# Thirty-four seven-product couples a layer in a two-layer encoder trunk, with block sums made by adding transfers

## The chip, the cores and the metric

One core of one Trainium2 chip runs the whole trunk in one launch. The metric is the time of an execution on the device in microseconds; the median of the runs counts, lower is better. Five engines work side by side: PE (matrix products), DVE (vector), ACT (scalar), POOL (GpSimd) and SP, which here only issues transfers. Each executes its own instructions in order and waits at semaphores for the others.

## The reference

The input is 256 tokens of width 2048, in float32. There are two layers. Layer 0 mixes tokens with a bidirectional mLSTM of 8 heads, layer 1 with a bidirectional gated linear recurrence (HGRN2) of 16 heads. After each mixer stands a ConvGLU of inner width 5504.

```python
def conv_glu(hn, w_up, conv_w, conv_b, w_down):
    u = hn @ w_up
    a, v = jnp.split(u, 2, axis=-1)
    ...
    return (jax.nn.gelu(c, approximate=False) * v) @ w_down

for layer in range(DEPTH):
    hn = rmsnorm(h, norm_mix_g[layer])
    ...
    h = h + mix
    h = h + conv_glu(rmsnorm(h, norm_ffn_g[layer]), ...)
return rmsnorm(h, final_g)
```

In `conv_glu`, `c` is `a` convolved over three neighbouring tokens, plus a bias. The change concerns the last product of `conv_glu`, 256 x 5504 by 5504 x 2048.

## The kernel before, in words

**Products.** Every float32 operand is split into a high and a low part (`wh`, `wl` for weights, two halves of a tile for activations), and a product is three matmuls: high by high, high by low, low by high. Weights come from DRAM in `raw` tiles of 2048 columns (1 MB, three buffers); `parts` makes pieces of 1024 columns from them, the high part by a copy on ACT, the low part by a subtraction on DVE. `stream` takes pieces three ahead of PE's use (LOOK).

**Chunks.** The work is a list of chunks. "fm" is 256 output features for all tokens, "tm" is 512 output features with the tokens as rows, "st" is a pair of such 512s.

**Pairs.** In a pair (`pair`, `squares_by_seven`), two 128-row slices of the contraction and two 512-column blocks form, with the two token halves, a product of 2 x 2 by 2 x 2 blocks. Such a couple takes eight products, or seven by a Strassen-like scheme (Winograd's form). The seven need sums of token blocks, which `token_sums` makes when the activation is produced, and sums T1 to T4 of weight blocks B11, B22, B21, B12. A pair holds all eight banks of PSUM: four for P1, P6, P7, P5 (`psm`), which `mid` adds to the residual after the last couple of seven, and four for C11, C12, C21, C22 (`psa`), which `done` adds at the end. `SEVEN` lists the couples of seven of the feed-forward stage, `SEVEN_MIX` those of the mixers' out projections, whose weight sums are made on the fly by DVE (`combine`).

**The feed-forward stage** (`ffn`) goes through its 43 tiles of inner width in two halves, of 22 (FA) and 21 (FB). Each half has one fm chunk per tile (`w_up`), whose `done_up` makes the activation tile. The first half then has two pairs, for output columns 0 to 1023 and 1024 to 2047, with 8 couples of seven each. The second half has one pair for columns 0 to 1023, with 6 couples of seven, and then two single tm chunks, for columns 1024 to 1535 and 1536 to 2047 (chunks 2 and 3, `w_d2`). That makes 22 couples of seven a layer. Their weight sums are made in the up chunks before them by `prepare`: it loads the four blocks into `pwh` and `pwl`, DVE does four operations of 512 columns, and the result goes to DRAM (`tscr`). `split_squares` later loads 768 KB of weights, 768 KB of sums into `T`, and 256 KB of sums into the free quarter of `raw`.

**Order.** Program order is written by generators. `Side` holds jobs, each with a due time on a clock that `tick` moves by 0.65 for each pair of matmuls in an fm chunk (10.4 a chunk of 16 slices) and by 1.3 for each slice of a tm chunk (20.8 a chunk of 16). A job's `yield 9.0` puts its next instructions 9 later on this clock. `until` and `drain` step the jobs at once, whatever their due time. A scheduler may still move instructions, except those that are pinned (`pin`, `late`), which keep their order. After out projection chunk 0 of a mixer, `mixed` calls `drain`.

**The norms.** `Norm.add(c)` squares the 512 columns of chunk c on ACT and pushes `turn(c)`, which transposes them on PE and makes four activation tiles `xt` for the next stage, one ACT and one DVE instruction each. `turn` waits while a pair holds the banks (`held`). The next stage's products start with tile 0 and take the tiles in order. The last norm (`FinalNorm`) scales and stores; `half` is its end, run for each token half inside the last chunk.

Of the kernel before, what the change touches and what calls it, by code (L numbers as in the profile page):

```python
# [46 lines left out]
LEAD = 48  # L47
TEMP = 3
GATES = 4 * AH
SEVEN = (1, 2, 3, 4, 6, 7, 8, 9), (1, 2, 4, 5, 7, 8)  # L50
# [6 lines left out]
C_ID, C_MF, C_MB, C_SUM, C_LV = 0, 128, 384, 640, 768  # L57
NCST = C_LV + FINE * QUAD


def trunk_kernel(ctx, tc, xT, x_d, fg_d, pp_d, cst_d, w_gate, w_first, w_aq, w_ak, w_av, w_ao, w_aout, w_ao2,
                 w_bq, w_bv, w_bg, w_bout, w_bo2, w_up, w_d0, w_d1, w_d2, out, mscr, tscr):
# [10 lines left out]
    cst = keep.tile([P, NCST], F32, name="cst")  # L73
# [45 lines left out]
    class Chunk:  # L119
        def __init__(self, kind, src, nk, x, done, before=None, last=False, swap=(), first=False, paced=False):  # L120
            self.last, self.swap, self.first, self.paced = last, swap, first, paced
            self.kind, self.src, self.nk, self.x, self.done, self.before = kind, src, nk, x, done, before
            self.width = {"fm": 256, "tm": 512, "st": 512}[kind]
# [57 lines left out]
    def split_squares(ch, parts):  # L181

        units, raws, kept = (ch.nk + 1) // 2, {}, {}
        side.until(lambda: ch.waits is None or ch.waits)
# [11 lines left out]
        def combine(u):  # L196
            r, T = raw(u), temporary(ch.pool, "T")
            B11, B22, B21, B12 = (r[:, j * 512:(j + 1) * 512] for j in range(4))
            T2, T3, T4 = (T[:, j * 512:(j + 1) * 512] for j in range(3))
            for x, y, out in ((B12, B22, T3), (B12, B11, B12), (B22, B12, T2), (B21, T2, T4)):  # L200
                dve.tensor_tensor(out, x, y, ALU.subtract)
            kept[u] = T
# [16 lines left out]
    def squares_by_seven(ch, fetch, ready):  # L219
# [18 lines left out]
        units, last = (ch.nk + 1) // 2, max(ch.seven)  # L238
        for u in range(units):
            fetch()  # L240
# [43 lines left out]
    def stream(chunks):  # L284
# [10 lines left out]
        for ch in chunks:  # L295
# [7 lines left out]
            while k < ch.nk:  # L303
                fetch()
                wh, wl, n = ready.pop(0)
                if ch.last and k + sum(p[2] for p in ready) + n == ch.nk:
                    pieces_, k0 = [(wh, wl, n)] + ready, k
                    for t in range(2):
                        k = k0
                        for wh, wl, n in pieces_:  # L310
                            for kk in range(n):
                                x, c = ch.x(k), slice(kk * 512, (kk + 1) * 512)
                                xh, xl = x[:, t * P:(t + 1) * P], x[:, T + t * P:T + (t + 1) * P]
                                pe.matmul(ps[t], xh, wh[:, c], start=False, stop=False)
                                pe.matmul(ps[t], xh, wl[:, c], start=False, stop=False)
                                pe.matmul(ps[t], xl, wh[:, c], start=False, stop=k == ch.nk - 1)
                                k += 1
                        ch.half(ps[t], t)
                    return
# [129 lines left out]
    class FinalNorm:  # L449
# [17 lines left out]
        def scale(self, c):  # L467
# [5 lines left out]
            if c == 2:  # L473
                ss = self.ss
                dve.tensor_tensor(ss[:, :, 0:1], ss[:, :, 0:1], ss[:, :, 1:2], ALU.add)
                dve.tensor_tensor(ss[:, :, 0:1], ss[:, :, 0:1], ss[:, :, 2:3], ALU.add)
                dve.tensor_scalar(self.rc, ss[:, :, 0], 1.0 / D, EPS, ALU.mult, ALU.add)

        def half(self, ps, t):
            side.drain()  # L480
            cs = slice(D - 512, D)
            h = hm[:, t, cs]
            dve.tensor_tensor(h, h, ps, ALU.add)
            last = keep.tile([P, 512], F32, tag=f"xt{4 + t}", name="fl")
            dve.scalar_tensor_tensor(last, h, 1.0, h, ALU.mult, ALU.mult, accum_out=self.ss[:, t, 3:4])
            rc = self.rc[:, t:t + 1]
            dve.tensor_scalar(rc, self.ss[:, t, 3:4], 1.0 / D, rc, ALU.mult, ALU.add)
            pool.tensor_tensor(rc, rc, hmx[:, 0:1], ALU.pow)
            for c in range(4):
                v = hm[:, t, 512 * c:512 * c + 512]  # L490
                if c in (1, 2):
                    act.activation(v, v, AF.Copy, scale=rc)
                elif c == 3:
                    dve.scalar_tensor_tensor(v, v, rc, self.g[3], ALU.mult, ALU.mult)
                else:
                    dve.tensor_scalar(v, v, rc, None, ALU.mult)
                (nc.scalar if c == 2 else nc.sync).dma_start(out[t, :, 512 * c:512 * c + 512], v)
# [11 lines left out]
    def project(wsrc, nk, x, norm):  # L509

        def done(c):
            def f_(ps):
# [3 lines left out]
                if norm is not None:  # L516
                    norm.add(c)
            return f_
        chunks = [Chunk("tm", wsrc(c), nk, x, done(c)) for c in range(4)]
        if isinstance(norm, FinalNorm):  # L520
            chunks[3].last, chunks[3].half = True, norm.half
        return chunks
# [6 lines left out]
    def token_sums(mp, i, a, b, S, last=None):  # L529
# [3 lines left out]
        for i, (x, y, op) in enumerate(((a[:, P:T], b[:, P:T], ALU.add), (a[:, P:T], a[:, 0:P], ALU.subtract),  # L533
                                        (S[:, 0:P], a[:, 0:P], ALU.subtract), (b[:, 0:P], S[:, 2 * P:3 * P], ALU.subtract))):
# [8 lines left out]
    def pair(src, nk, c0, x, sums, norm, seven):  # L543
# [5 lines left out]
        def mid(ps):  # L549
# [6 lines left out]
            dve.tensor_tensor(part(0, 1), part(0, 1), u, ALU.add)  # L556
            dve.tensor_tensor(part(1, 1), part(1, 1), P5, ALU.add)
            dve.tensor_tensor(u, u, P7, ALU.add)  # L558
            pool.tensor_tensor(part(1, 0), part(1, 0), u, ALU.add)  # L559
            pool.tensor_tensor(part(1, 1), part(1, 1), u, ALU.add)  # L560

        def done(ps):
            for i in range(4):
# [12 lines left out]
        ch.stored, ch.waits, ch.pool = {}, None, None  # L576
        return ch

    def prepare(mp, todo, period, finished):
# [13 lines left out]
        for i, (_, dst) in enumerate(todo):  # L593
# [3 lines left out]
            for x, y, out in ((B12, B22, B22), (B12, B11, B12), (B11, B22, B11), (B21, B11, B21)):  # L597
                dve.tensor_tensor(out, x, y, ALU.subtract)  # L598
# [3 lines left out]
        finished.append(True)  # L602
# [33 lines left out]
    def mlstm(norm, nxt):  # L636
# [10 lines left out]
        def load(loaded, follower):  # L647
# [26 lines left out]
            late(cst[:, 0:C_LV], cst_d[:, 0:C_LV])  # L674
# [8 lines left out]
        def begin():  # L683
            c = stack.enter_context(tc.tile_pool(name="cols", bufs=1))
            box["cc"] = c.tile([P, 2, H], F32, name="cc")
            box["emn"] = c.tile([P, 2, H], F32, name="emn")
            mp = box["mp"] = stack.enter_context(tc.tile_pool(name="ml", bufs=1))
# [5 lines left out]
        def gates(gs):  # L693
            with tc.tile_pool(name="gt", bufs=1) as gp:
# [3 lines left out]
                pe.matmul(pg[:, 0:T], cst[:, C_SUM:C_SUM + P], gs, start=True, stop=True)  # L698
# [45 lines left out]
        segs = [  # L744
            (0, 256, 0, 0, 0, cst[:, C_MF:C_MF + 256]),
            (256, 384, 1, 0, 128, cst[:, C_MF:C_MF + 128]),
            (384, 512, 0, 1, 0, cst[:, C_MB + 128:C_MB + 256]),
            (512, 768, 1, 1, 0, cst[:, C_MB:C_MB + 256]),
        ]

# [8 lines left out]
        def weights(hd):  # L759
# [6 lines left out]
            for lo, hi, s, dr, t0, mk in segs:  # L766
# [5 lines left out]
        def head(st, j):  # L772
# [7 lines left out]
            for lo, hi, s, dr, t0, mk in segs:  # L780
# [132 lines left out]
    def hgrn(norm, nxt):  # L913
# [4 lines left out]
        def begin():  # L918
            mp = box["mp"] = stack.enter_context(tc.tile_pool(name="hg", bufs=1))
            late(cst[:, C_LV:], cst_d[:, C_LV:])  # L920
# [193 lines left out]
    def ffn(layer, norm, nxt):  # L1114
        stack = ExitStack()
        box = dict(n=(2 * len(SEVEN[0]) + len(SEVEN[1])) * layer)
        chunks, pairs = [], []
# [9 lines left out]
        def done_up(f, i, GT, SX, seven):  # L1127
            def go(ps):
# [18 lines left out]
                if i % 2 and i // 2 in seven:  # L1147
                    n = seven.index(i // 2)
                    if seven is SEVEN[0]:
                        z = GT[i - 1][:, P:T], GT[i - 1][:, T + P:2 * T]  # L1150
                    else:
                        if n % 3 == 0:
                            box["s4"] = mp.tile([P, 768], F32R, tag=f"sx{len(seven) + n // 3}", name="s4")
                        z = tuple(box["s4"][:, (n % 3 * 2 + j) * P:(n % 3 * 2 + j + 1) * P] for j in range(2))
# [4 lines left out]
        for part, (f0, nf) in enumerate(((0, FA), (FA, FB))):  # L1159
            GT, SX, todo, finished = [], {}, [], []  # L1160

            def prep(todo=todo, finished=finished, nf=nf):
                if not pairs[0].pool:
                    begin()
                side.push(prepare(box["mp"], todo, (nf * 10.4 - 26.0) / len(todo), finished))

            for i in range(nf):
                chunks.append(Chunk("fm", w_up[layer, f0 + i], KT, norm.x, done_up(f0 + i, i, GT, SX, SEVEN[part]),
# [146 lines left out]
```

## Time and profile before

| | |
|---|---|
| median of 3 runs | 2397.41 us |
| the runs | 2397.41, 2397.83, 2393.29 us |
| span of the profiled execution, first to last instruction | 2388.1 us |
| what lies around the span, against the median | 9.3 us |
| PE busy | 2371.3 us, 99% |
| DVE busy | 1939.6 us, 81% |
| ACT busy | 1352.4 us, 57% |
| POOL busy | 189.7 us, 8% |
| moved by DMA | 578.15 MB, mean 242 GB/s |

The profile is of one execution; the times of its parts are read against its own span. A row of a group gives the count, the busy time and the mean duration of one, then the idle time of the engine before them and what ended it. A row of waits gives the total, how often and the longest. A row of the chain or of the timeline gives its start, its length and how many instructions it merges. PE's granted clock is full in nearly all of the span, 0.999 in the mean.

### The profile page before, as it was taken

To read this page: it belongs to the slowest core of one execution; us is meant where nothing else is said; L and a number is where in the kernel's file an instruction comes from. 1 tells how busy PE (TensorE), PEld (TensorE's weight loads), DVE (VectorE), ACT (ScalarE), POOL (GpSimd) and SP (SyncE) were. 2 spreads that over 40 slices of the span, in tenths; PEclk is the share of its full clock that TensorE was granted. 3 is DMA by queue.
4 is the path that set the end of the run, shared out by engine and by line. 5 is a ranking of instruction groups with operands and counts; after the bars stand their busy time and mean duration, and the time that the engine had idled before them with its cause. 6 is when DMAs were issued, how large, how long until landed. Compare 5 with 4: busy or idle time off the path is not lost.

```text
span 2388.1 us, 38126 instructions
## 1 busy us (share of the span) xinstructions
PE 2371.3 (99%) x14596; PEld 2027.1 (85%) x14596; DVE 1939.6 (81%) x3167; ACT 1352.4 (57%) x2141; POOL 189.7 (8%) x240
## 2 busy tenths in 40 slices
PE   9999999999999999999999999999999999999998
PEld 7888888888788888888888888888888878888887
DVE  7766687888888888767888989889788888888874
ACT  7655455555565555655555555556555566455563
POOL 0100000000000000001222222220000000000000
PEclk9999999999999999999999999999999999999999
DMA  8654546998987777755544554545798998777774
GB/s 301 201 183 163 185 184 226 324 322 323 330 340 277 271 247 242 277 190 182 177 162 175 177 175 164 175 173 190 277 324 326 333 359 310 265 244 249 246 273 143
DMA packets 105703, 578.15 MB, mean 242 GB/s; under 512 B 11936, under 2 KB 12448, under 8 KB 58672
## 3 DMA queue, kind: packets, MB, share of 16 engines
q1 hardware_dynamic: 103824, 571.71, 67.5%
q0 software_dynamic: 1120, 3.21, 0.7%
q8 instruction: 114, 1.87, 0.3%
q10 hardware_dynamic: 576, 0.79, 0.1%
q14 instruction: 69, 0.57, 0.1%
HBM read 527.37 MB, written 48.30 MB: 241 GB/s over the span
## 4 chain that ended last, share of the span: by engine, by line
PE 90%; DMA 6%; DVE 3%; issue 1%; ACT 0%; SPq 0%; POOLq 0%; POOL 0%; DVEq 0%; ACTq 0%
PE mm L330 32%; PE mm L346 23%; PE mm L334 16%; PE pc L229 10%; PE mm L229 5%; DMA pwl<-in_w_d 2%; DVE wl L143 1%; DMA T<-tscr 1%; DMA pwh<-in_w_d 1%; PE pn L793 1%; PE py L1051 1%; DMA tscr<-pwl 1%; PE pd L1001 0%; PE pz L407 0%; PE pa L1001 0%
## 5 line engine op out<-in xcount | busy, mean ns | idle before, releaser
L330 PE MATMUL mm<-xt,wh 128*128 128x512 f32 x3776 | 1314.0, 394 | 0.0
L143 DVE TENSOR_TENSOR wl<-raw,wh 128x1024 fp32r<-128x1024 f32 (+1 forms) x846 | 1033.4, 1227 | 268.7 <-ACT wh L142 265.3
L142 ACT CAST wh<-raw 128x1024 fp32r<-128x1024 f32 (+1 forms) x846 | 874.4, 1040 | 567.1 <-PE mm L330 265.6
L334 PE MATMUL mm<-xt,wl 128*128 128x256 f32 x3776 | 1046.6, 278 | 1.1 <-DVE wl L143 1.1
L330 PEld LDWEIGHTS mm<-xt,wh 128*128 128x128 f32 x3776 | 706.2, 188 | 159.3
L334 PEld LDWEIGHTS mm<-xt,wl 128*128 128x128 f32 x3776 | 709.5, 188 | 6.5 <-DVE wl L143 2.0
L346 PE MATMUL mm<-wh,xt 128*128 128x512 f32 x1024 | 320.6, 391 | 1.8 <-ACT xt L352 1.3
L346 PEld LDWEIGHTS mm<-wh,xt 128*128 128x128 f32 x1024 | 191.5, 188 | 42.0 <-ACT xt L352 1.7
L346 PE MATMUL mm<-wl,xt 128*128 128x512 f32 x512 | 198.2, 391 | 0.0
L229 PE MATMUL pc<-wh,g 128*128 128x512 f32 x576 | 195.1, 390 | 0.3 <-ACT wh L142 0.2
L229 PEld LDWEIGHTS pc<-wh,g 128*128 128x128 f32 x576 | 108.0, 188 | 24.8 <-ACT wh L142 2.0
L229 PE MATMUL pc<-wl,g 128*128 128x512 f32 x288 | 112.3, 390 | 0.9 <-DVE wl L143 0.9
L346 PEld LDWEIGHTS mm<-wl,xt 128*128 128x128 f32 x512 | 96.2, 188 | 18.9
L143 DVE TENSOR_TENSOR wl<-T,wh 128x1024 fp32r<-128x1024 f32 (+1 forms) x100 | 93.8, 951 | 21.7 <-ACT wh L142 21.3
L229 PE MATMUL mm<-wh,sx 128*128 128x512 f32 x300 | 107.1, 391 | 2.8 <-ACT wh L142 2.8
L142 ACT CAST wh<-T 128x1024 fp32r<-128x1024 f32 (+1 forms) x100 | 82.3, 835 | 45.7 <-PE pc L229 23.3
L559 POOL TENSOR_TENSOR hm<-hm,u 128x512 f32<-128x512 f32 x8 | 11.2, 1399 | 1151.6 <-DVE u L558 1151.6
L1138 ACT ACTIVATE avc<-avc,pp 128x256 f32<-128x256 f32 x86 | 51.6, 600 | 87.7 <-DVE avc L1136 87.7
L346 PE MATMUL mm<-wh,g 128*128 128x512 f32 x308 | 96.5, 392 | 0.0
L1133 ACT COPY avc<-mm 128x256 f32<-128x256 f32 x172 | 63.7, 371 | 51.4 <-PE mm L334 50.9
L598 DVE TENSOR_TENSOR pwl<-pwl 128x512 f32<-128x512 f32 x88 | 60.2, 684 | 27.9 <-DMA pwl<-in_w_d 27.9
L598 DVE TENSOR_TENSOR pwh<-pwh 128x512 f32<-128x512 f32 x88 | 60.2, 684 | 27.8 <-DMA pwh<-in_w_d 21.6
(256 smaller groups left out, 2504.3 us busy)
## 6 DMA issues: line engine op xcount, KB each, us to landing
raw<-in_w_up SPq DMA_DIRECT2D x172, 1024.0 KB, 6.1
raw<-in_w_bq SPq DMA_DIRECT2D x48, 1024.0 KB, 4.9
raw<-in_w_d SPq DMA_DIRECT2D x40, 1024.0 KB, 5.2
raw<-in_w_d SPq DMA_DIRECT2D x44, 768.0 KB, 6.7
T<-tscr SPq DMA_DIRECT2D x44, 768.0 KB, 8.0
raw<-in_w_ao SPq DMA_DIRECT2D x24, 1024.0 KB, 4.6
pwh<-in_w_d SPq DMA_DIRECT2D x44, 512.0 KB, 8.1
pwl<-in_w_d SPq DMA_DIRECT2D x44, 512.0 KB, 7.7
```

The costliest lines, as they stand in the source:

```text
L142: pin(act.copy(wh[:, :m], r))
L143: pin(dve.tensor_tensor(wl[:, :m], r, wh[:, :m].bitcast(F32), ALU.subtract))
L229: pe.matmul(ps, a, b, start=id(ps) not in begun, stop=stop and i == 2)
L330: pe.matmul(ps[f], wh[:, c:c + P], x, start=k + kk == 0, stop=False)
L334: pe.matmul(ps[f][:, 0:T], wl[:, c:c + P], x[:, 0:T], start=False, stop=k + kk == ch.nk - 1)
L346: pe.matmul(ps[t], x[:, a + t * P:a + (t + 1) * P], w[:, c], start=st and i == 0, stop=sp and i == 2)
L559: pool.tensor_tensor(part(1, 0), part(1, 0), u, ALU.add)
L598: dve.tensor_tensor(out, x, y, ALU.subtract)
L793: pe.matmul(pn[:, 0:258], w, v, start=(i == 0), stop=(i == len(parts) - 1))
L1051: pe.matmul(py[:, c], AT[:, s if s == t else 2 + s], V[:, s, j * P:(j + 1) * P], start=(s == 0), stop=(s == 1))
L1133: act.copy(z, p[:, T:2 * T])
L1138: act.activation(c, a, AF.Identity, bias=col("conv_b", layer * FT + f), scale=cw[1])
```

## The change

The first half's two pairs have 9 couples of seven instead of 8 each. The second half's chunks 2 and 3 become a pair as well, and both its pairs have 8 couples of seven, the first one instead of 6. That makes 34 a layer. The last couple of the last pair of all, and the single slice after it, are taken bank by bank (`tail`), and `FinalNorm.bank` replaces `half`.

Of the 34 couples, four (couple 5 of each pair, `FLY`) are summed on the fly. The sums of the other 30 are stored in DRAM. The first 14 of them are made during the mixer before (`prepare_by_transfers`): a copy of the four blocks in DRAM on SP's queue, then four transfers from POOL's queue that add in DRAM, where T2 reads T3's result and T4 reads T2's. These are pinned. 9 are made by DVE in the first half's up chunks, 7 in the second half's. Signs change so that every sum is an addition. Each pair waits only for its own sums. `done` adds C11, C21, C12, C22 in this order. The mLSTM's masks leave the kept constants and are loaded when the mLSTM begins, into memory that the start-up held.

```diff
-SEVEN = (1, 2, 3, 4, 6, 7, 8, 9), (1, 2, 4, 5, 7, 8)
+SEVEN = (1, 2, 3, 4, 5, 6, 7, 8, 9), (1, 2, 3, 4, 5, 6, 7, 8)
+FLY = 5
+STORED = 2 * (len(SEVEN[0]) + len(SEVEN[1]) - 2)
+BY_TRANSFERS = 14
+FIRST = 9
+PERIOD = 28.0
...
-        side.until(lambda: ch.waits is None or ch.waits)
+        side.until(lambda: not ch.waits)
...
+        def tail(u):
+            fetch()
+            p, q, r = (ready.pop(0)[:2] for _ in range(3))
+            x0, x1, x2 = (ch.x(2 * u + i) for i in range(3))
+            ws = ((block(p, 0), block(q, 0), block(r, 0)), (block(q, 1), block(p, 1), block(r, 1)))
+            for i, ps in enumerate(psa_):
+                for x, w in zip((x0, x1, x2), ws[i % 2]):
+                    product(ps, half(x, i // 2), w, x is x2)
+                ch.bank(ps, i)
...
-            for i in range(4):
+            for i in (0, 2, 1, 3):
                 h = part(i // 2, i % 2)
                 dve.tensor_tensor(h, h, ps[i], ALU.add)
...
+    def prepare_by_transfers(todo):
+        def unit(src, dst, left):
+            late(dst, src)
+            T2, T3, T4, T1 = (dst[:, j * 512:(j + 1) * 512] for j in range(4))
+            B11, B12 = src[:, 0:512], src[:, 1536:2048]
+            yield 12.0
+            for out, in_ in ((T3, B12), (T1, B11), (T2, T3), (T4, T2)):
+                tc.keep_in_program_order(pool.dma_start(out, in_, accum_op=ALU.add))
+                if out is not T3:
+                    yield 9.0
+            left.pop()
+        for job in todo:
+            while held:
+                yield 1.0
+            side.push(unit(*job))
+            yield PERIOD
...
+            masks = box["masks"] = c.tile([P, NCST - NKEPT], F32, name="masks")
+            late(masks, cst_d[:, NKEPT:])
...
+                jobs = todo[BY_TRANSFERS:][0:FIRST] if part == 0 else todo[BY_TRANSFERS + FIRST:]
+                side.push(prepare(box["mp"], jobs, (nf * 10.4 - 26.0) / len(jobs)))
...
+            for c0, src in ((0, w_d0[layer][:, f0 * 1024:(f0 + nf) * 1024]), (2, w_d1[layer][:, f0 * 1024:(f0 + nf) * 1024])):
+                ch = pair(src, nf, c0, lambda k, GT=GT: GT[k], lambda u, SX=SX: SX[u], nxt if part else None, seven)
+                ch.waits = []
                 for u in seven:
+                    if u != FLY:
+                        ch.stored[u] = tscr[box["n"]]
+                        ch.waits.append(True)
+                        todo.append((src[:, 2048 * u:2048 * (u + 1)], tscr[box["n"]], ch.waits))
...
-                chunks += project(lambda c: w_d2[layer, c % 2], nf, lambda k, GT=GT: GT[k], nxt)[2:]
...
-    c, close0 = ffn(0, n1, n2)
+    c, close0, chunks[2].before = ffn(0, n1, n2)
...
-    c, close1 = ffn(1, n3, nf)
+    d, close1, c[1].before = ffn(1, n3, nf)
```

165 lines of the change are left out of this document (68 added, 97 removed).

## The prediction

> **What bounds the kernel now.** I read the page's head first, then the waits of PE, the chain, the windows by stage, and last the places that the change touches.
>
> ```profile
> span 2388.1 us, 38126 instructions
> PE 2371.3 (99%) x14596; PEld 2027.1 (85%) x14596; DVE 1939.6 (81%) x3167; ACT 1352.4 (57%) x2141; POOL 189.7 (8%) x240
> PE 90%; DMA 6%; DVE 3%; issue 1%; ACT 0%; SPq 0%; POOLq 0%; POOL 0%; DVEq 0%; ACTq 0%
> PE mm L229 <- ACT wh L142: 2.8, 2, 1.5
> PE mm L346 <- ACT xt L352: 1.3, 1, 1.3
> 743.92 5.89 PE pc L229 x26
> 1073.07 22.69 PE mm L346 x100
> ```
>
> PE is busy for 2371.3 of 2388.1 us; only 16.8 us are not matmul, and the largest wait of PE in total is 2.8 us. So work taken from PE pays in full, if nothing else comes late. What one matmul costs is read from the chain and not from its mean duration (390 ns, which overlaps the next): 100 in 22.69 us and 26 in 5.89 us, 0.227 us each.
>
> The stages, by window (us, then busy time and count of PE, PEld, DVE, ACT, POOL, then granted clock, DMA share, GB/s):
>
> ```profile
> 0.00:300.00 300.00, 297.43 (x1715) 252.51 (x1716) 208.50 (x387) 179.71 (x303) 15.93 (x37) 1.00 0.60 207
> 323.00:370.00 47.00, 47.00 (x209) 38.94 (x208) 45.18 (x63) 26.75 (x33) 3.54 (x2) 1.00 0.54 195
> 394.00:636.00 242.00, 240.91 (x1388) 209.96 (x1387) 207.26 (x343) 131.52 (x209) 0.00 (x0) 1.00 0.90 319
> 636.00:691.00 55.00, 52.72 (x231) 42.62 (x231) 47.55 (x57) 38.94 (x49) 0.00 (x0) 1.00 0.97 367
> 691.00:746.00 55.00, 54.91 (x242) 45.16 (x241) 47.04 (x49) 34.30 (x39) 4.35 (x2) 1.00 0.84 303
> 978.00:1033.00 55.00, 55.00 (x251) 45.79 (x250) 42.83 (x50) 34.12 (x43) 0.00 (x0) 1.00 0.76 273
> 1033.00:1061.00 28.00, 28.00 (x133) 23.19 (x132) 18.07 (x23) 15.27 (x26) 3.55 (x2) 1.00 0.50 173
> 1090.00:1588.00 498.00, 497.70 (x4472) 429.23 (x4471) 434.21 (x889) 273.72 (x520) 138.11 (x175) 1.00 0.50 174
> 1611.00:1657.00 46.00, 46.00 (x205) 38.09 (x204) 45.27 (x66) 25.54 (x32) 2.52 (x2) 1.00 0.54 197
> 1920.00:1980.00 60.00, 58.10 (x255) 45.96 (x254) 51.66 (x64) 41.44 (x52) 0.00 (x0) 1.00 0.96 367
> ```
>
> In order: the mLSTM heads, its paired out projection, the first half's up chunks of layer 0, its two pairs, the second half's pair and then one single chunk, the HGRN heads, its paired out projection, and the first pair of layer 1. PE is full everywhere but in the first pair of each layer: 2.3 us missing at 636 and 1.9 at 1920, where the DMA engines are at 0.97 and 0.96. The mixers have DMA to spare (0.60 and 0.50).
>
> **1. Products removed.** A couple in seven products instead of eight saves one, which is three matmuls. First half: 9 instead of 8 couples in each of two pairs, 2 saved. Second half: the pair goes from 6 to 8, 2 saved; chunks 2 and 3 now take 21 x 6 x 2 = 252 matmuls, as a pair 8 x 7 + 2 x 8 + 4 = 76 products or 228, which is 8 products less. 12 a layer, 24 in all: 72 x 0.227 = **-16.3 us**. This is PE time with nothing behind it.
>
> **2. The boundary between layer 0 and the HGRN.** Today the norm's transposes and tiles of columns 0 to 1023 run under single chunk 2, those of chunk 2 under chunk 3, and only chunk 3's are late. After, the second pair holds all of them until it ends, because a turn waits while a pair has the four banks. So 16 tiles are made at the moment when the next chunk wants them.
>
> ```profile
> 1072.25 0.82 PE L407 MATMUL pz<-cst,hm 128*128 128x128 f32 x6
> 1095.38 0.39 PE L346 MATMUL mm<-wh,g 128*128 128x512 f32 x1
> 1095.60 0.39 PE L330 MATMUL mm<-xt,wh 128*128 128x512 f32 x1
> 1101.51 0.84 ACT L352 ACTIVATE xt<-pz,pp 128x256 fp32r<-128x256 f32 x2 [0.42 <-PE pz L407]
> L353 DVE SCALAR_TENSOR_TENSOR xt<-pz,pp,xt 128x256 fp32r<-128x256 f32 x48 | 21.4, 478 | 3.1 <-ACT xt L352 3.1
> L501 ACT ACTIVATE jk<-hm 128x512 f32<-128x512 f32 x38 | 23.9, 630 | 3.1 <-POOL hm L560 1.6 <-DVE hm L565 0.3 <-DVE hm L515 0.3
> ```
>
> Now there is no gap: the last matmul of chunk 3 starts at 1095.38, the next chunk's first at 1095.60. After, the first tile takes transposes (0.82 for six), ACT 0.42 and DVE 0.48, with two hand-overs, about 2.5 us of idle PE. Then the tiles must keep up: the chunk lasts 242 / 22 = 11.0 us, and ACT owes 16 x 0.42 = 6.7, four squares of 0.63, 2.5, and four weight casts of about 1.04 (page: 874.4 us for 846), 4.2: 13.4 us, 2.4 over. Between 2 us (squares put off) and 9 (DVE's four additions and splits before the first tile as well); I take **+4**, near the sum of 2.5 and half of 2.4.
>
> **3. Pair after pair.** A pair's first product needs the bank of the previous pair's C11. That hand-over exists at 695 us:
>
> ```profile
> 695.80 0.19 PEld L229 LDWEIGHTS pc<-wh,g 128*128 128x128 f32 x1 [0.52 <-DVE hm L565]
> 656.67 2.35 DVE L143 TENSOR_TENSOR wl<-raw,wh 128x1024 fp32r<-128x1024 f32 x2
> 658.94 0.68 DVE L143 TENSOR_TENSOR wl<-T,wh 128x512 fp32r<-128x512 f32 x1
> 659.54 1.22 DVE L143 TENSOR_TENSOR wl<-raw,wh 128x1024 fp32r<-128x1024 f32 x1
> L598 DVE TENSOR_TENSOR pwl<-pwl 128x512 f32<-128x512 f32 x88 | 60.2, 684 | 27.9 <-DMA pwl<-in_w_d 27.9
> ```
>
> It costs 0.52 us; two new ones, and C12 now evicted third: **+1** (0 to 3).
>
> **4. DVE inside the pairs.** Back to back, DVE needs 1.135 us for a split of 1024 columns (2.27 from 656.67 to 658.94) and 0.60 for 512. A couple of seven asks three and one, 4.0 us, against 21 x 0.227 = 4.76 of PE. In the pair at 691, DVE goes from 47.04 by one couple's extra split (1.135 + 0.60) and by the couple that is now summed on the fly (four additions of 0.60) to 51.2, with PE at 54.3: 94%. The two out projections run at 45.18 of 47 and 45.27 of 46 with PE full, so 94% can be borne. But a couple on the fly wants 6.4 us of DVE in 4.76 of PE, once in each of eight pairs. **+2** (0 to 8, the last if each waits its 1 us).
>
> **5. Sums prepared by DVE.** Down from 22 to 16 a layer, 9 of them in the first half's up chunks, where there were 16: 7 x 4 x 0.60 = 17 us less DVE and 7 x 2 MB less traffic in a window at 0.90. The first pair then finds its sums stored long ago, and the 2.3 and 1.9 us missing there can shrink: **-2.5** (-4 to 0). The traffic of the new second pair, 7 x 1.79 + 3.5 MB in about 52 us, is some 315 GB/s where the single chunks drew 173; the 367 at 636 shows room, at nothing, with up to 3 us in the bound of step 4.
>
> **6. Sums made by transfers.** For each of 14 couples a layer: one 1 MB copy in DRAM on SP's queue, then four accumulating transfers of 256 KB from POOL's queue, each chained one waiting for the one before (T2 for T3, T4 for T2). 14 x 2 MB over some 280 us (from 43, the gate products and one chunk later, to 323) adds about 105 GB/s to the 207 of the mLSTM, and 59 to the HGRN's 174. No row shows an accumulating transfer; the nearest:
>
> ```profile
> fg<-in_fg POOLq DMA_DIRECT2D x4, 256.0 KB, 8.0
> Mb<-mscr POOLq DMA_DIRECT2D x16, 128.0 KB, 6.0
> raw<-tscr SPq DMA_DIRECT2D x44, 256.0 KB, 7.3
> 63.50 2.18 POOL L764 DMA_DIRECT2D Mb<-mscr  x4 [1.68 <-DMA mscr<-M]
> 366.28 1.29 POOL L559 TENSOR_TENSOR hm<-hm,u 128x512 f32<-128x512 f32 x1 [61.20 <-DVE u L558]
> ```
>
> The fourth row shows POOL itself standing until an earlier transfer has landed, before it issues; behind it stand, in order, the powers of the head norms, in the HGRN the gate products, and DVE waits for those. The program puts 9 us between chained transfers. At 8.0 us, the row of the same size and queue, POOL need not stand. The Trainium skill, "DMA: Bandwidth & Descriptors", section "Anatomy of one DMA — SWDGE (gpsimd) path", fits a GpSimd-issued transfer as 2.0 us plus bytes over 436 GB/s; an estimate by it is 2.6 us for 256 KB, the sum would be the same and the margin wide, and these rows, at 6 to 8 us, do not agree.
>
> One place has no 9 us. In side time the mLSTM offers 10.4 + 20.8 + 3 x 62.4 + 20.8 = 239 from where the transfers begin to the end of out chunk 0, and 14 x 28 = 392 are wanted; the drain at the end of that chunk sends the last five copies at once and the rest of the accumulations in a row. Five copies at 367 GB/s are 14 us in front of the paired projection's weights, of which two loads, about 11 us of PE, are already ahead: 3 us. The row of eight chained steps at 6 to 8 us is 48 to 64 us of POOL from about 312, and POOL's addition at 366.28 must follow. The HGRN offers 426 and is not drained. For all of it **+3** (0 to 25).
>
> **7. Start and end.** The masks go into memory that the start-up holds until the gate products have run.
>
> ```profile
> 29.54 1.93 PE L870 MATMUL pq<-gx,wg 128*32 128x256 f32 x32
> 41.09 0.60 PE L698 MATMUL pg<-gs,cst 128*128 128x256 f32 x2
> cst<-in_cst SPq DMA_DIRECT2D x1, 384.0 KB, 9.8
> 2379.83 0.68 DVE L483 TENSOR_TENSOR hm<-hm,mm 128x512 f32<-128x512 f32 x1
> ```
>
> Issued at 31.5, landed after 9.8 us, at 41.3, wanted at 41.09: **+0.3** (0 to 2). The end keeps its chain of addition, square, power, scaling and store, from 2379.83 to 2388.1; banks finish one by one, and one scaling moves from a plain multiply to one with a second operand: 0, within 1 either way. The new signs move no time.
>
> **Sum.** -16.3 + 4 + 1 + 2 - 2.5 + 3 + 0.3 = -8.5 us. The span would be 2379.6; the median of the three runs, 2397.41, lies 9.3 us over the span and keeps that, so 2388.9.
>
> **Rivals.** *All of it covered*: the tiles of step 2 come in time but for 2 us, the burst of step 6 is swallowed, 5 holds: about -15, 2382. For it: PE's waits are nearly nothing today though DVE is at 90% in places. Against: step 2 has no cover left.
> *The gain is turned into waits* in the mLSTM's drain and in the pairs: the second ends of steps 4 and 6 in part, 8 us more, 2397, no change. For it: eight steps of 8 us reach past 366, and an addition of DVE waits for POOL there.
> *POOL stands in the HGRN*, the slower side. If a chained accumulation takes L over 9 us, POOL stands 28 x (L - 9) us over 14 couples; DVE, which waits for POOL's products, has 498 - 434 = 64 us to spare. From L = 9 + (64 + 8.5) / 28 = 11.6 us the gain is gone; at 12 it is 84 - 64 = 20 us against 8.5, 2409. For it: an accumulation reads two operands and writes, in DRAM, beside loaded queues. Against: 8.0 us for 256 KB. The same page's section "Two DMAs through the same engine are not ordered" says that the issuing engine has to wait for the earlier transfer's semaphore; the row at 63.50 agrees.
> *The sums are not there in time*: then the pairs' loads wait behind accumulations; the drains exclude it in the program's order, so it is priced with the last.
>
> **Chances.** Forecast 0.45 (2384 to 2393), all covered 0.15, turned into waits 0.20, POOL standing 0.20. What this measurement tells from no change is about 0.2%, 4.8 us. Faster (under 2392.6) 0.60, within 0.20, slower 0.20. The range reaches from 2379, all covered and step 5 in full, to 2406, and leaves out most of the last case.
>
> **What would show it.** PE instructions down by 72; the two pairs of a second half together 2 x 52 us; after the second pair a gap of 3 to 5 us ahead of the first HGRN chunk, ended by ACT or DVE on xt; the first pairs without their 2 us; the accumulations landing in 6 to 8 us, POOL busy but not standing, PE full in the HGRN. Wrong would be: accumulations over 11 us, POOL's rows in the HGRN ended by a DMA, DVE idle for POOL, or PE idle in the paired out projection of the mLSTM.

## The result, and the profile after

The change made the kernel slower. Its median is 2432.74 us against 2395.35 for the kernel before on the same chip, a ratio of 1.0152 with a 95% interval of 1.0128 to 1.0175. The profiled execution took 2423.3 us with a span of 2421.5, 33.4 longer than the span before. The forecast was 2388.9 us, with a range of 2379 to 2406.

About 2 us lie around the span in every execution on record. Most of the 9.3 us that the table of the time before puts there are something else: the execution that was profiled took some 2390 us and was shorter than the median. The trace after is of the shortest of its four executions as well. So the parts below sum to +33.4, while the medians differ by 37.4.

The head of the page after:

```profile
span 2421.5 us, 38387 instructions
PE 2372.3 (98%) x14524; PEld 2022.9 (84%) x14524; DVE 2002.2 (83%) x3244; ACT 1392.3 (57%) x2201; POOL 291.8 (12%) x356
PE 84%; DMA 6%; DVE 5%; issue 2%; POOL 1%; ACT 1%; SPq 0%; POOLq 0%; DVEq 0%; ACTq 0%
```

The 72 matmuls are gone (14596 to 14524), and yet PE is as busy as before: matmuls after a stall run longer (up to 775 ns instead of 481 in the rows below). PE's part of the chain falls from 90% to 84%.

The two out projections are found by the tiles that only they read, `ya` (mLSTM) and `yb` (HGRN). The rows give the count, the shortest, median and longest duration in ns, then the first and last start in us. Before:

```profile
L346 PE MATMUL mm<-wh,ya x128: 387/389/481, 300.7 to 389.2; 128*128 128x512 f32 x128
...
L346 PE MATMUL mm<-wh,yb x128: 387/389/481, 1584.9 to 1677.7; 128*128 128x512 f32 x128
```

After:

```profile
L353 PE MATMUL mm<-wh,ya x128: 387/389/775, 302.7 to 423.5; 128*128 128x512 f32 x128
...
L353 PE MATMUL mm<-wh,yb x128: 387/389/498, 1622.3 to 1715.2; 128*128 128x512 f32 x128
```

The mLSTM's out projection took 88.5 us and takes 120.8. That alone is +32.3 of the 33.4. The HGRN's is unchanged (92.8 and 92.9).

The windows after, with the columns of the prediction: the mLSTM's out projection, the first pair of layer 0, the HGRN heads, the first pair of layer 1.

```profile
302.70:423.50 120.80, 96.72 (x408) 76.68 (x407) 72.81 (x105) 51.44 (x76) 27.07 (x32) 0.89 0.91 244
668.00:771.50 103.50, 103.50 (x460) 85.75 (x459) 94.70 (x106) 73.09 (x85) 3.54 (x2) 1.00 0.88 320
1121.00:1622.00 501.00, 494.59 (x4439) 424.25 (x4440) 432.40 (x879) 271.61 (x521) 186.23 (x230) 1.00 0.75 222
1960.00:2020.00 60.00, 60.00 (x268) 49.71 (x267) 55.13 (x63) 40.44 (x49) 3.55 (x2) 1.00 0.90 340
```

In the first row PE is missing 24 us, the DMA engines are at 0.91 and the granted clock at 0.89. The first pairs, rows two and four, are full now. The HGRN misses 6.4 us of PE, where it missed 0.3.

The boundary, from the timeline of PE after (start, length, and what ended the idle time before):

```profile
1117.30 0.39 PE L236 MATMUL pc<-wh,g 128*128 128x512 f32 x1
1117.91 2.54 PE L414 MATMUL pz<-cst,hm 128*128 128x128 f32 x16 [0.23 <-DVE hm L568]
1121.49 0.50 PE L337 MATMUL mm<-xt,wh 128*128 128x512 f32 x1 [1.04 <-DVE xt L360]
...
1124.54 0.50 PE L337 MATMUL mm<-xt,wh 128*128 128x512 f32 x1 [2.08 <-DVE xt L360]
```

From the pair's last product to the HGRN's first, 4.2 us pass, of which 2.54 are sixteen transposes. Another tile is 2.08 us late.

With these starts every kernel divides into the same five stretches: to the first `ya` product, the mLSTM's out projection (to the last `ya` product), layer 0's feed-forward stage (to the HGRN's first product on `xt`), the HGRN heads (to the first `yb` product), and the rest. All numbers are differences of starts in the trace, in us.

| kernel | to out proj. | out proj. | FFN 0 | HGRN | rest |
|---|---|---|---|---|---|
| before | 300.7 | 88.5 | 706.4 | 489.3 | 803.2 |
| after | 302.7 | 120.8 | 698.0 | 500.8 | 799.2 |
| e1_dve_all | 301.1 | 88.5 | 724.4 | 494.8 | 816.6 |
| e2_hgrn_only | 301.3 | 88.5 | 725.8 | 502.7 | 798.0 |
| e3_spread | 311.1 | 89.3 | 698.2 | 503.5 | 800.1 |
| e4_unchained | 308.8 | 111.9 | 698.8 | 500.0 | 797.8 |
| e5_small_sums | 301.6 | 97.6 | 699.0 | 503.3 | 799.3 |
| e6_no_sums | 301.4 | 98.0 | 700.2 | 494.8 | 798.0 |
| e7_eight | 303.3 | 89.9 | 699.4 | 500.1 | 795.2 |
| e8_eight_slow | 303.0 | 90.6 | 699.5 | 499.0 | 800.0 |
| e9_eight_early | 305.2 | 89.1 | 703.8 | 494.3 | 796.2 |
| e10_early_tiles | 303.5 | 89.2 | 705.6 | 490.4 | 796.3 |

So +33.4 is: the mLSTM +2.0, its out projection +32.3, layer 0's feed-forward stage -8.4, the HGRN +11.5, the rest -4.0.

One trace stands for each kernel, and a stage with the same program isn't equally long in two of them: the HGRN takes 500.8, 502.7 and 503.5 in after, e2 and e3, FFN 0 698.0 to 700.2 in after and e3 to e6, and the rest differs by 4.8 between e7 and e8. Smaller differences say nothing.

What happens in the out projection is in the waits between 300 and 424 us after (total, times, longest):

```profile
POOL tscr L590 <- DMA tscr<-tscr: 43.7, 7, 11.2
POOL tscr L590 <- DMA tscr<-in_w_d: 32.2, 6, 14.5
...
DVE T L208 <- DMA raw<-in_w_ao: 18.8, 2, 15.9
...
DVE hm L568 <- POOL hm L562: 13.5, 1, 13.5
...
PE pz L414 <- DVE hm L568: 10.0, 1, 10.0
PE mm L236 <- ACT wh L149: 9.0, 2, 8.5
```

and in the timeline of SP and POOL there:

```profile
311.08 3.37 SPq L375 DMA_DIRECT2D tscr<-in_w_d  x5
...
402.54 0.81 POOL L590 DMA_DIRECT2D tscr<-tscr  x1 [0.20 <-issue]
403.09 1.55 POOL L562 TENSOR_TENSOR hm<-hm,u 128x512 f32<-128x512 f32 x1
```

These are step 6's five copies at the drain, and the row of accumulations on POOL behind them. DVE waits up to 15.9 us for the projection's weights `in_w_ao`, and POOL's addition, at 366.28 before, stands behind the accumulations until 403.09. Of the 32.3 us, 24.1 are idle PE (120.80 less 96.72), 8.5 of them in one wait for weights and 10.0 in one behind POOL's addition. The other 8.2 are the same products at a lower clock: it was 0.51 between 340 and 350 us and 0.57 between 400 and 410.

### The profile page after: what moved, and what is told of

It is laid out like the page before. It is cut to its first block, busy times and chain, and to the rows that moved or that the text cites. A ratio compares the mean times of both kernels' runs of the same rounds, so it can differ in the third digit from the quotient of the medians.

```text
span 2421.5 us, 38387 instructions
## 1 busy us (share of the span) xinstructions
PE 2372.3 (98%) x14524; PEld 2022.9 (84%) x14524; DVE 2002.2 (83%) x3244; ACT 1392.3 (57%) x2201; POOL 291.8 (12%) x356
## 3 DMA queue, kind: packets, MB, share of 16 engines
q1 hardware_dynamic: 105264, 588.49, 69.2%
## 4 chain that ended last, share of the span: by engine, by line
PE 84%; DMA 6%; DVE 5%; issue 2%; POOL 1%; ACT 1%; SPq 0%; POOLq 0%; DVEq 0%; ACTq 0%
PE mm L337 35%; PE mm L341 18%; PE mm L353 11%; PE pc L236 10%; PE mm L236 7%; DMA tscr<-in_w_d 3%; DVE wl L150 2%; DMA tscr<-tscr 2%; DVE kq L1015 1%; DMA T<-tscr 1%; PE pn L816 1%; DMA raw<-in_w_d 1%; PE py L1073 1%; DVE QK L1035 1%; DVE QK L1036 0%
## 5 line engine op out<-in xcount | busy, mean ns | idle before, releaser
L236 PE MATMUL pc<-wh,g 128*128 128x512 f32 x696 | 238.0, 390 | 0.0
L236 PE MATMUL mm<-wh,sx 128*128 128x512 f32 x444 | 158.0, 392 | 0.5 <-ACT wh L149 0.5
L236 PEld LDWEIGHTS pc<-wh,g 128*128 128x128 f32 x696 | 131.1, 188 | 27.5
L150 DVE TENSOR_TENSOR wl<-T,wh 128x1024 fp32r<-128x1024 f32 (+1 forms) x148 | 141.4, 966 | 13.4 <-ACT wh L149 13.1
L149 ACT CAST wh<-T 128x1024 fp32r<-128x1024 f32 (+1 forms) x148 | 122.5, 835 | 51.2 <-DMA T<-tscr 14.4
L236 PE MATMUL pc<-wl,g 128*128 128x512 f32 x348 | 135.7, 390 | 0.0
L236 PEld LDWEIGHTS mm<-wh,sx 128*128 128x128 f32 x444 | 83.9, 189 | 18.3 <-ACT wh L149 0.9
L236 PE MATMUL mm<-wl,sx 128*128 128x512 f32 x222 | 87.3, 393 | 0.6 <-DVE wl L150 0.6
L1156 DVE TENSOR_TENSOR avc<-mm,avc 128x256 f32<-128x256 f32 x172 | 72.1, 419 | 13.9 <-ACT avc L1155 13.7
L1015 DVE COPY kq<-QK 128x256 f32<-128x256 f32 x224 | 76.4, 361 | 4.2 <-POOL QK L988 4.2
```

What stands on the lines that cost most here:

```text
L149: pin(act.copy(wh[:, :m], r))
L150: pin(dve.tensor_tensor(wl[:, :m], r, wh[:, :m].bitcast(F32), ALU.subtract))
L236: pe.matmul(ps, a, b, start=id(ps) not in begun, stop=stop and i == 2)
L1015: dve.tensor_copy(m[:, j].rearrange("k (m p j) -> k m p j", p=2, j=h), blocks(z, h, 0, T))
L1156: dve.tensor_tensor(z, p[:, 0:T], z, ALU.add)
```

## The experiments

**Who prepares the sums.** e1_dve_all gives all 30 sums to DVE; e2_hgrn_only keeps the transfers for layer 1 only.

```diff
-BY_TRANSFERS = 14
-FIRST = 9
+BY_TRANSFERS = 0
+FIRST = 16
```

> All 30 stored sums of a layer are made by DVE in the up chunks (16 before the first half's pairs, 14 in the second half's), none by transfers; couples, pairs and everything else as in the changed kernel. Theory A (the loss is the transfers: the drained burst in the mLSTM's out projection, about 32 us, and the HGRN, about 11): 2378 to 2390, the out projection of the mLSTM back at 88.5 us and the HGRN heads at 489 to 493. Theory B (the transfers' bytes slow the weights wherever they run): the same here. Theory C (the longer pairs themselves cost, by DVE or by DMA): over 2400, with PE idle in the pairs.

Measured: 2427.46 us, 1.0143 (1.0116 to 1.0170). The out projection is back at 88.5, so the transfers cause its loss. But the time is theory C's and not theory A's: the feed-forward stage of layer 0 takes 724.4, 26.4 more than with transfers, and the rest 17.4 more. The waits of PE in e1:

```profile
PE pc L236 <- DVE wl L150: 11.2, 8, 6.8
PE mm L236 <- ACT wh L149: 6.5, 6, 3.0
PE mm L341 <- DVE wl L150: 5.8, 8, 1.9
```

DVE's splits come late inside the pairs and in the up chunks. What the transfers take off DVE is real: 14 more sums a layer on DVE cost 43.8 us here, where step 5 had valued seven fewer in each first half at 2.5. This also means that "undo the transfers" is not the remedy.

```diff
-                jobs = todo[BY_TRANSFERS:][0:FIRST] if part == 0 else todo[BY_TRANSFERS + FIRST:]
+                by, first = ((0, 16), (BY_TRANSFERS, FIRST))[layer]
+                jobs = todo[by:][0:first] if part == 0 else todo[by + first:]
...
-        return chunks, stack.close, lambda: side.push(prepare_by_transfers(todo[:BY_TRANSFERS]))
+        return chunks, stack.close, lambda: side.push(prepare_by_transfers(todo[:(0, BY_TRANSFERS)[layer]]))
```

> Transfers only during the HGRN (14 sums of layer 1); layer 0's 30 sums by DVE. Theory A: the mLSTM's 32 to 34 us are gone, the HGRN's 11 stay: 2390 to 2402. Theory B: half of the bytes, half of the loss: about 2408.

Measured: 2417.08 us, 1.0095 (1.0065 to 1.0125). Each layer behaves by its own preparer: out projection 88.5 and FFN 0 at 725.8 as in e1, HGRN 502.7 and the rest 798.0 as after. The time lies above both forecasts, since both took layer 0's sums on DVE to be free.

**The burst itself.** e3_spread issues a unit every 14.5 of side time in the mLSTM, not 28, so that almost nothing is left for the drain.

```diff
-            yield PERIOD
+            yield every
...
-        return chunks, stack.close, lambda: side.push(prepare_by_transfers(todo[:BY_TRANSFERS]))
+        return chunks, stack.close, lambda: side.push(prepare_by_transfers(todo[:BY_TRANSFERS], (14.5, PERIOD)[layer]))
```

> As the changed kernel, but in the mLSTM a unit of transfers begins every 14.5 instead of every 28 of the program's clock, so that all 14 are issued before the drain; the HGRN keeps 28. Theory A (the burst at the drain is the cost): the out projection falls from 120.8 us to 89 to 94 us and the time to 2398 to 2408. Theory B (the bytes): the same bytes in a shorter time, 2428 to 2440, the loss moved ahead into the heads.

Measured: 2398.55 us, 1.0016 (1.0001 to 1.0032). The same transfers, spread, leave the out projection at 89.3, which shows that the burst is the cause. But the heads before it take 8.4 us longer than after. POOL's waits between 60 and 310 us in e3:

```profile
POOL tscr L590 <- DMA tscr<-tscr: 97.5, 11, 10.6
POOL tscr L590 <- DMA tscr<-in_w_d: 52.3, 12, 9.4
```

and in the same stretch after:

```profile
POOL tscr L590 <- DMA tscr<-in_w_d: 55.4, 9, 11.3
...
POOL tscr L590 <- DMA tscr<-tscr: 24.3, 5, 8.8
```

At the faster rate POOL stands before its accumulations for 150 of 250 us, where it stood for 80: the mechanism of the third rival, in the other mixer. The trace has a path for most of the 8.4 us. POOL stood 9.42 us before two accumulations and issued the next loads of `Mb` at 84.94 (after: 4.89 us, at 81.82). DVE then waited 5.03 us for `Mb`, PE 5.6 for ACT's `rd` behind it (0.8 after), and the granted clock was 0.96 between 100 and 150 us (1.00 after). That this standing is what slows the heads was not tried by itself. The execution traced in e3 is the longest of its ten, 5.5 us over the median, so that other executions may lose less there.

**Three parts of the burst.** e6_no_sums leaves the accumulations out and keeps the copies; e5_small_sums has them move 16 columns each; e4_unchained lets T2 and T4 read weights and not sums.

```diff
-                tc.keep_in_program_order(pool.dma_start(out, in_, accum_op=ALU.add))
+                pass
```

> As the changed kernel, with the copies but no accumulations at all (the sums are left out). Theory B2: HGRN heads at 495 here and at 500 or more with small accumulations. Theory B3 (the copies on SP's queue cost): 499 or more here too. Out projection of the mLSTM: what five copies in a row cost by themselves, 100 to 110 us by theory A (14 us of copies less the cover, with a slow clock after the stall), 89 to 92 if the accumulations make all of it.

```diff
-                tc.keep_in_program_order(pool.dma_start(out, in_, accum_op=ALU.add))
+                tc.keep_in_program_order(pool.dma_start(out[:, 0:16], in_[:, 0:16], accum_op=ALU.add))
```

> As the changed kernel, with the same 56 accumulating transfers a layer, chained and from POOL, but each of 16 columns instead of 512 (nearly all of the sums is left out): 8 KB instead of 256. The copies stay. Theory B1 (the accumulations' bytes cost): HGRN heads fall from 501 to about 495, what they take without any transfers; out projection of the mLSTM from 121 to 105 to 112. Theory B2 (POOL's issuing costs: 0.8 to 1.1 us each, in the way of the HGRN's gate products): HGRN stays at 500 to 504.

```diff
-            for out, in_ in ((T3, B12), (T1, B11), (T2, T3), (T4, T2)):
+            for out, in_ in ((T3, B12), (T1, B11), (T2, B12), (T4, B11)):
```

> As the changed kernel, but T2 and T4 add a block of weights instead of T3 and T2 (this leaves out one addend of the second and two of the fourth sum of 14 couples a layer), so that no transfer waits for another accumulation; bytes, count and the drain stay. Theory A1 (in the burst POOL stands from accumulation to accumulation, and its addition for the residual comes 37 us late): the stall of 10 us at the addition goes, the stalls ahead of it for weights stay: 2410 to 2425. Theory A2 (five copies ahead of the weights in SP's queue are nearly all of it): 2428 to 2436. HGRN: if POOL's standing is its cost, 489 to 494 us instead of 500.8; if not, as it is.

Measured: e6 2394.35 us, 0.9998 (0.9986 to 1.0010); e5 2402.89, 1.0036 (1.0023 to 1.0048); e4 2411.85, 1.0072 (1.0047 to 1.0097).

In the out projection, the copies alone cost 9.5 us (98.0 against 88.5). The issuing of the accumulations adds nothing (97.6), chained as it is there. At full size, with the chain, they add the other 23 (120.8). Without the chain it is 111.9, but the mLSTM before it is 6.1 us longer in e4, so the projection ends only 2.8 us earlier than after (420.7 against 423.5). By these two traces the chain counts for 3 to 9 us and the bytes for most of it.

The times say otherwise. e4's trace is of the longest of its five executions, 7.7 us over the median, and after's of the shortest of four, 9.4 under it. By the ratios (1.0152 and 1.0072) the chain is worth about 19 us, and what is left between e4 and e5 about 9. In e4's trace PE's wait of 10.0 us behind POOL's addition is gone, as theory A1 said, and the longest wait for weights is 15.7 instead of 8.5. So both the bytes and the chain count, the chain only where its transfers are large; how the 23 us divide between them stays open.

In the HGRN the parting is another. Without accumulations it takes 494.8, with small ones 503.3, with unchained ones 500.0, with the real ones 500.8. The differences among the last three are no larger than among traces of the same HGRN, so neither bytes nor chain show there; that POOL issues accumulations does. POOL's groups between 1090 and 1640 us, which holds the HGRN, before and then after (busy us, mean ns, idle time before):

```profile
L1019 POOL TENSOR_TENSOR G<-G 128x384 f32<-128x384 f32 (+2 forms) x96 | 67.8, 707 | 6.3
```

```profile
L1041 POOL TENSOR_TENSOR G<-G 128x384 f32<-128x384 f32 (+2 forms) x96 | 76.9, 801 | 5.0
...
L590 POOL DMA_DIRECT2D tscr<-in_w_d x28 | 23.8, 1001 | 0.2 <-issue 0.2
L590 POOL DMA_DIRECT2D tscr<-tscr x28 | 23.5, 841 | 41.6 <-DMA tscr<-in_w_d 22.5 <-DMA tscr<-tscr 13.6 <-DVE QK L1036 5.3
```

the same group in e6 and in e5:

```profile
L1041 POOL TENSOR_TENSOR G<-G 128x384 f32<-128x384 f32 (+2 forms) x96 | 67.8, 706 | 6.3
```

```profile
L1041 POOL TENSOR_TENSOR G<-G 128x384 f32<-128x384 f32 (+2 forms) x96 | 80.8, 842 | 4.9
```

and DVE's copies of `kq` before and after:

```profile
L993 DVE COPY kq<-QK 128x256 f32<-128x256 f32 x214 | 67.2, 338 | 0.0
```

```profile
L1015 DVE COPY kq<-QK 128x256 f32<-128x256 f32 x210 | 72.8, 366 | 4.2 <-POOL QK L988 4.2
```

An issue occupies POOL for 0.84 to 1.00 us in the mean, 47.3 us in all, and in that stage POOL's gate products take 13% longer and DVE's copies 8%. POOL stood 36.1 us before chained accumulations (22.5 + 13.6), and e4, where that standing is gone, gains 0.8, which is less than the spread. The Trainium skill, "SBUF — State Buffer", section "Who interferes with whom", says that DVE and GpSimd share one pair of ports, that a DVE copy can hold it, and that GpSimd needs it to write the descriptors of its transfers. The two rows on `kq` are in line with it, 338 ns and 366 beside the issues, but show only that copies take longer, not a port that is held. The path to PE can be read in part, from the waits in the HGRN after:

```profile
DVE kq L1015 <- POOL QK L988: 4.2, 3, 2.4
PE pa L1047 <- DVE QK L1036: 2.0, 3, 1.1
```

DVE's copies wait for POOL's gate products, and PE's score products (`pa`) for DVE. Neither wait stands in the traces before, in e1, e6 or e9, which have no accumulations in the HGRN. But PE's waits that name DVE, DMA or the splits there sum to about 3 us; where the other 3 arise isn't settled.

**Fewer transfers.** e7_eight makes 8 sums a layer by transfers, which fits into the side time before the drain, and gives DVE 11 in each half. e8_eight_slow also issues them every 48 in the HGRN.

```diff
-BY_TRANSFERS = 14
-FIRST = 9
+BY_TRANSFERS = 8
+FIRST = 11
```

> 8 sums a layer by transfers instead of 14, so that the mLSTM's all begin before the drain (8 x 28 = 224 of 239); DVE makes 11 in each half's up chunks. Theory A: out projection at 89 to 91, mLSTM heads at 302, the HGRN at 498, the pairs as in the changed kernel: 2380 to 2392, faster than before. Rival (DVE's preparation has no room beside the longer pairs, as where it made all): pairs of the first half over 112, and 2395 to 2410.

> As the one with 8 sums a layer by transfers, but a unit every 48 of the program's clock in the HGRN. If the HGRN's cost is a matter of the rate (bytes at once), its heads come to 495 to 497; if each transfer has its price, the same as at 28, and the time within 3 us of it.

Measured: e7 2391.68 us, 0.9989 (0.9975 to 1.0002); e8 2392.17, 0.9985 (0.9970 to 1.0000). The out projection is at 89.9 and 90.6, so the burst is gone, and DVE bears two more sums in a first half and four more in a second (FFN 0 at 699.4). Both intervals reach 1.0000 or beyond, so a time below that before isn't shown. The HGRN takes 500.1 and 499.0 with 32 accumulations, against 500.8 to 503.5 with 56: the rate makes no difference that shows, and the traces are too few to say whether the price goes with the number.

**Elsewhere.** e9_eight_early issues layer 1's eight during layer 0's up chunks, and e10_early_tiles also makes tiles 0 to 7 of the next norm between the two pairs of layer 0's second half.

```diff
-    d, close1, c[1].before = ffn(1, n3, nf)
+    d, close1, first_up[2].before = ffn(1, n3, nf)
```

> The edit: eight units a layer are summed by transfers, as in e7_eight, and DVE prepares the others (11 in a first half's pairs); layer 1's eight are issued during layer 0's up chunks, from the third one on, one unit each 48 of paced work, and none in the HGRN. Theory A (POOL's issuing of the 56 and 32 accumulations is what lengthens the HGRN, its clocks and the rest of the layer being as they were): the HGRN falls from 500.1 us in e7_eight to 494 to 496, as in the two runs without sums there; layer 0's up chunks keep their 245.6 and 241.4 within 2 us, since POOL has few other instructions there; the time is 2384 to 2389, that is faster than before. Theory B (the HGRN is longer because its tiles come late from the boundary, the sums add nothing): the HGRN stays at 500 and the time at 2391 to 2393. Theory C (the accumulations lengthen whatever stage they stand in): the HGRN falls by 5 and layer 0's up chunks grow by as much, the time stays at 2391 to 2393.

```diff
+                if part and c0 == 0 and isinstance(nxt, Norm):
+                    ch.after = lambda: side.until(lambda: nxt.xs[7] is not None)
```

> The edit: e9_eight_early, and before the second pair of layer 0's second half begins, the side work is driven on until tiles 0 to 7 of the next norm are made, so that the first transposes of the HGRN find their tiles. Theory A (the late tiles at layer 0's end cost the gap and the extra length of the HGRN's beginning): from the last product of layer 0 to the end of the HGRN is shorter by 3 to 5 us, the hand-over between the two pairs longer by 3 to 4; the time is within 2 us of e9_eight_early. Theory B (the boundary's cost is the pair's own tail, its additions after the last product, which no earlier tile can shorten): nothing is gained at the boundary, and the hand-over between the pairs costs 3 to 4: the time is 3 to 4 us above e9_eight_early.

Measured: e9 2388.58 us, 0.9979 (0.9966 to 0.9992); e10 2387.24, 0.9966 (0.9954 to 0.9979). Both are faster than the kernel before, by 0.2 and 0.3%. In e9 the HGRN falls from 500.1 to 494.3 and the time is in theory A's range. But FFN 0 grows from 699.4 to 703.8, so that in the traces three quarters of the gain go again. Theory C would have it all in the up chunks; they take 247.6 and 241.5 us, where e7 had 245.6 and 241.4, and the other half of the growth is in the pairs, where no accumulation is issued. What lengthens these was not tried. The intervals of e7 and e9 overlap, so that the early place is the better one isn't shown by the times. In e10, from the timeline of PE:

```profile
1098.05 0.39 PE L236 MATMUL pc<-wh,g 128*128 128x512 f32 x1
1098.28 0.39 PE L339 MATMUL mm<-xt,wh 128*128 128x512 f32 x1
```

The gap (4.2 us after, 4.4 in e9) is gone, and the HGRN is 3.9 shorter, at 490.4 against 489.3 before: together twice what theory A said. But FFN 0, in which the eight tiles are now made, is 1.8 longer although it has lost the gap. That leaves 2.1 us; the medians differ by 1.3 and their intervals overlap. What is shown is that late tiles made the gap and most of the HGRN's slow beginning, and not that making them earlier gains anything on the whole.

## Why the prediction was wrong, point by point

**Step 6 failed, by its drain.** The place, the five copies and the row of accumulations reaching past 366 us were foreseen; the term was sized at +3, with 25 as its end, and measured 32.3. Three things were mis-sized. The copies were priced as 14 us less 11 of weights ahead, 3; they cost 9.5. The row of accumulations was priced as eight steps, 48 to 64 us of POOL; POOL waited 13 times for 75.9 us (43.7 + 32.2), and came to its addition at 403 and not at 360 to 376. And the accumulations were priced only as time on POOL, not as traffic. What traffic they are shows between 0 and 300 us, after and then in e6 (copies only):

```profile
0.00:300.00 300.00, 296.61 (x1706) 251.25 (x1707) 207.37 (x377) 178.09 (x298) 39.30 (x65) 1.00 0.82 257
```

```profile
0.00:300.00 300.00, 296.85 (x1712) 251.87 (x1713) 208.17 (x385) 178.92 (x302) 16.07 (x37) 1.00 0.68 235
```

Before stood 0.60 and 207 GB/s. Copies add 28 GB/s for 0.08 of the engines, 350 GB/s for the whole of them; accumulations add 22 for 0.14, 157. A counted byte of an accumulation holds the engines about 2.2 times as long, in the packet time that the share counts. The queues of the whole execution agree: SP's moves 588.49 MB in 69.2% of the engines' time after, 351 GB/s, and POOL's 29.37 MB more than in e6 in 8.2% more of the time, 148 GB/s. The size of the pieces doesn't explain it: between 0 and 300 us after, a packet of 2 KB takes 207 ns in an accumulation and 91 in a plain load from DRAM. In the window of the burst:

```profile
330.00:380.00 50.00, 35.89 (x131) 26.54 (x130) 31.24 (x50) 18.65 (x22) 9.95 (x12) 0.83 0.95 239
```

The engines are nearly as full (0.95) as in the first pair before (0.97), but at 239 GB/s and not 367. I had the second number as the room that the burst would find. The Trainium skill, "DMA: Bandwidth & Descriptors", section "Issuing engines are not separate DMA queues", says that transfers of all issuing engines interleave on the same 16. The trace agrees: DVE waited 8.3 us for SP's weights with the copies alone (e6), and 15.9 with POOL's accumulations beside them.

**The other part of step 6 failed too: the HGRN.** It was put at nothing, because POOL need not stand at 8.0 us for 256 KB. That estimate held:

```profile
tscr<-in_w_d POOLq DMA_DIRECT2D x56, 256.0 KB, 8.0
tscr<-tscr POOLq DMA_DIRECT2D x56, 256.0 KB, 6.7
```

But the question was the wrong one: not how long they take to land, but what 56 issues of 0.9 us do to the engines beside them. That cost 6.0 of the 11.5 us (500.8 against 494.8 in e6); by which mechanism is shown only in part.

**The rivals.** *POOL stands in the HGRN* gave the sign but neither place nor mechanism: the median landing stayed under 9 us, and without the standing that there was (e4) the HGRN took 500.0. POOL stood in the mLSTM's out projection instead. *Gain turned into waits* had the right place, the mLSTM's drain, and 8 us for it. The slower side deserved its chance under the drain, with a price from DMA occupancy. *All of it covered* failed at the drain. Of the signs of being wrong that were named, two came: PE idle in the mLSTM's out projection, and POOL's rows in the HGRN ended by a DMA.

**Step 1 held**: 72 matmuls fewer. **Steps 3, 4 and 5** are best seen with the products in layer 1's feed-forward stage, where no boundary follows: the rest fell 4.0 us, and of that the out projection takes +0.1 and the end +2.7, so the stage gained 6.7. The steps' half share there was -8.2 + 0.5 + 1 - 1.2 = -7.9. Layer 0's stage gained 12.4, its -8.4 without the 4.0 by which the gap grew. Together that is 19.1 where the steps had 15.8. Step 5's stalls are gone as said, with the windows at 668 and 1960 full.

**Step 2**: +4 was taken, 9 its end. The gap grew by 4.0 (0.2 to 4.2), and without accumulations the HGRN is 5.5 longer than before (e6), of which e10 shows 3.9 to be the late tiles. So the boundary cost 7.9 to 9.5 us, twice the value taken and about the end of its range. The idle gap was foreseen; the second tile, 2.08 us late, and the lower clock behind it (0.97 in the HGRN's first 50 us) were not.

**Step 7**: the start was +0.3, and in e1 and e6, which have no accumulations, the first out projection starts 0.4 and 0.7 us later than before. The end was put at 0. From the last product's start to the end it was 9.0 us (2379.09 to 2388.1) and is 11.7 (2409.85 to 2421.5): the four banks' additions and squares now come in one row on DVE after the last products, where a half was done before.

```profile
2409.49 0.68 DVE L489 TENSOR_TENSOR hm<-hm,pc 128x512 f32<-128x512 f32 x1
...
2414.41 1.42 DVE L503 SCALAR_TENSOR_TENSOR hm<-hm,fss,fg 128x512 f32<-128x512 f32 x2 [0.67 <-POOL fss L497]
```

Against the sum, in the trace: products, pairs and sums together came out 3 us better than said; the drain missed by 29, the HGRN's issues by 6, the boundary by about 5 and the end by 3.

## What to carry to other kernels

When a schedule has a drain, work out how much of the paced work is still open there, and price the rest as traffic in front of what comes next, in DMA time and not in bytes. Work that is taken from one engine and given to transfers costs the issuing engine and its neighbours; choose a stage where that engine has little to do, and read how much that stage gives back (in e9's trace 4.4 of 5.8 us). Before stages of two traces are compared, look at where each traced execution lies among its kernel's times. Splitting a suspected cost into copies, issues, bytes and chain by four small edits told more than any view of the whole; where their traces and their times disagree, as in e4, the share is open.

## What the runs showed of the hardware

An accumulating transfer of 256 KB within DRAM lands after 6.7 to 8.0 us in the median (7.6 to 9.7 in e3, where they come faster), but a counted byte of it holds the DMA engines about 2.2 times as long as one of a plain copy (157 against 350 GB/s for the whole of the engines). Its issue takes POOL 0.84 to 1.00 us in the HGRN, and in e5, where it moves 8 KB, no less (0.87 to 0.99). Beside such issues POOL's products grew from 707 to 801 ns and DVE's copies from 338 to 366. After PE had waited 8.5 us in the out projection, its granted clock was 0.51 between 340 and 350 us and 0.83 between 330 and 380, so that single products took up to 797 ns instead of 389: a stall costs more than its own length.
